# Sparse attention on one core: products with the values issued for two key tiles at a time, with PSUM divided anew

## The chip, the core and the metric

The kernel runs on one of the eight cores of a Trainium2 chip. The metric is the device time of one execution in microseconds. A core has five engines with an instruction queue each: TensorE (PE in the profile; its weight loads are PEld) for matrix products, VectorE (DVE), ScalarE (ACT) and GpSimd (POOL) for work on tiles, and SyncE (SP), which here issues DMAs. Each runs its queue in order and waits at semaphores for the others. TensorE writes its results to PSUM, which here is handed out in eight banks of 128 partitions by 512 float32; the other engines read them from there and free the bank.

## The reference

One inference step of a decoder layer with two head groups: native sparse attention (8 query heads of 64, 2 key/value heads) and a gated DeltaNet, under one norm, one input projection and one output projection. There are 2048 prompt tokens of width 1024 and 8 x 4 sample tokens. For the attention of the prompt, which is where the change is:

```
s  = q_raw . ck / 8 ; p = softmax(s, c_start + 31 <= q_pos) ; o_cmp = p . cv          # compressed blocks
imp = p . overlap ; idx = top_8(imp, first block and the two at the query forced)     # 64-token blocks
o_slc = softmax(q . k over the 8 chosen blocks, causal) . v                           # selected blocks
o_win = softmax(q . k, 0 <= q_pos - k_pos <= 512) . v                                 # sliding window
o = (g0 * o_cmp + g1 * o_slc + g2 * o_win) * silu(z)
```

Every float32 product of the projections and scores is made of split parts; the outputs are float32.

## The kernel before

The program is written with a tile framework: the Python code names tiles and operations, and a scheduler fixes the order of each engine's queue when the kernel is built. It goes by the order in which the code issues the operations, by when operands and buffers are free in its own timing, and it places every semaphore wait. So an order on an engine is the scheduler's, and not always that of the code.

The stages are `project`, `gdn`, `nsa` (the attention) and `outproj`; parts overlap at their edges. `nsa` works through 8 units, `units`: 4 query blocks `qs` of 512 queries times 2 key/value heads `h`. For each unit there are three branches `b` (0 compressed, 1 selected, 2 window) and two pairs `p` of query heads. In branch 1 the selection is not gathered: all keys are scored, and rows of the operand `QHM` carry a large negative number for the blocks that were not chosen and the negative row maximum.

`stream` makes one flat list, `items`, of key tiles `(k, b, p, n, N, x)`: unit, branch, pair, number, count and the key tile of 128 keys with its columns of queries. For an item:

- `score` (lines 1469 to 1497) makes, for each of two heads, a tile pss of PSUM with two matmuls (`scores`, lines 1440 and 1441), and ScalarE takes the exponential into a tile pt of SBUF (line 1482). Where the tile crosses the diagonal or the window's edge, VectorE masks 128 columns (line 1492).
- the product with the values (line 1573) takes pt into the accumulator O, 64 output rows for each head, side by side in the two halves of TensorE's columns. It is a float32 product; the trace shows it in two passes, so a key tile has four rows. The first of the two also waits until both heads' pt are ready.
- pt is added to the pt of the pair's first key tile, on VectorE or GpSimd by the running counts in `busy` (line 1583), for the softmax's sum. After the pair's last key tile ScalarE copies O to oS (line 1587), and `defer` lines up `sums` (tile L) and the `merge` steps, which scale the three branches (tile B, line 1528) and add them on GpSimd (lines 1532 and 1541) some items later.

The scores run `dep` = 1 item ahead of the products. After each item `stream` yields, and the loop at the end of `nsa` issues some steps of `prepare` for the next unit: the compressed branch's maxima and scores (psc, psr), the choice of blocks (psl, psp, psi, tsel), and the maxima that the exponentials need. For these TensorE scores the keys once more, into psm (line 1374, with a mask addition in line 1376), psw (1389 and 1390) and psv (1397 and 1399), and VectorE reduces each to block maxima (lines 1377, 1391 and 1400). At a unit's end `max_end` puts these together (tile wm, lines 1403 to 1406), and `max_rows` transposes wm on TensorE (tile tm, line 1283) and sends it by DMA into rows of `QHM`, before the next unit's scores. Just before the first item of the next unit is scored, `stream` yields "last" and the rest of `prepare` is issued.

PSUM's eight banks are divided by `pb3 = 2, 3, 3`: two for O, three for the scores (pss, psr), three for everything that `X` hands out (psm, psw, psv, psc, psl, psp, psi, tsel, tm, L, B). `npt` = 8 buffers hold pt, `nos` = 9 hold oS.

Of the kernel before, what the change touches and what calls it, by code (L numbers as in the profile page):

```python
# [7 lines left out]
F32 = mybir.dt.float32  # L8
# [3 lines left out]
AF = mybir.ActivationFunctionType  # L12
ALU = mybir.AluOpType
# [91 lines left out]
class K:  # L105
# [1100 lines left out]
    def nsa(self):  # L1206
        nc, tc, i, o = self.nc, self.tc, self.i, self.o
        with ExitStack() as st:
# [262 lines left out]
            def score(u, b, p, item):  # L1471

                kt, c0, c1, mk = item
                if b == 0:
                    return [u["pc"][2 * p], u["pc"][2 * p + 1]]
                out = []
                for g in (2 * p, 2 * p + 1):
                    ps = pS.tile([128, 512], F32, tag="s", name="pss")
                    scores(ps[:, c0:c1], key(KHH, b - 1, u["h"], kt, kt + 1), key(KLM, b - 1, u["h"], kt, kt + 1),
                           u["QHL"][:, g, c0:c1], u["QHM"][:, g, c0:c1])  # L1480
                    pt = wk.tile([128, 512], F32, tag="pt", name="pt", bufs=self.npt)
                    last = nc.scalar.activation(pt[:, c0:c1], ps[:, c0:c1], AF.Exp)  # L1482
# [12 lines left out]

            def sums(u, b, W):

                L = X([128, 512], "L")
                for g in range(4):
                    nc.tensor.matmul(L[32 * g:32 * g + 32, :], self.ones[:, 0:32], W[g], start=True, stop=True, tile_position=(0, 32 * g))  # L1500
                t = wk.tile([128, 512], F32, tag="T", name="T", bufs=1)
                nc.scalar.activation(t, L, AF.Copy)
                nc.sync.dma_start(u["Ld"][b], t[0:128:32, :])
# [41 lines left out]
            def stream():  # L1545

                items = []
                for k, (qs, h) in enumerate(units):
                    for b in range(3):
                        for p in range(2):  # L1550
                            t = tiles_of(qs, b)
                            items += [(k, b, p, n, len(t), x) for n, x in enumerate(t)]
                W = {}

                def ahead(j):
                    if j < len(items):
                        k, b, p, n, N, x = items[j]
                        W[j] = score(U[k], b, p, x)
                for j in range(self.dep):
                    ahead(j)  # L1560
                for j, (k, b, p, n, N, x) in enumerate(items):
                    u = U[k]
                    e = j + self.dep
                    if e < len(items) and items[e][0] != items[e - 1][0]:
                        yield "last", items[e - 1][0]
                    ahead(e)
                    kt, c0, c1, mk = x
                    if n == 0:
                        O = pO.tile([128, 512], F32, tag="O", name="O")
                        acc = W[j]  # L1570
                    val = cvP[:, 64 * u["h"]:64 * u["h"] + 64] if b == 0 else V[b - 1, kt // 4][:, kt % 4, 64 * u["h"]:64 * u["h"] + 64]
                    for gg in range(2):
                        mm = nc.tensor.matmul(O[64 * gg:64 * gg + 64, c0:c1], val, W[j][gg][:, c0:c1], start=(n == 0), stop=(n == N - 1), tile_position=(0, 64 * gg))  # L1573
                        if gg == 0 and len(W[j]) == 3:

                            tc.add_manual_dep(mm.ins, W[j][2].ins.name, mybir.DependencyInfo(mybir.DependencyClass.Sync, mybir.DependencyReason.DATA), reason="both heads at once")
                    if n:
                        for gg in range(2):
                            w = (c1 - c0) / 512
                            tp_, td = 0.1 + self.nb[0] * w, 0.1 + self.nb[1] * w  # L1580
                            e = "p" if busy["p"] + tp_ <= busy["d"] + td else "d"
                            busy[e] += tp_ if e == "p" else td
                            (nc.gpsimd if e == "p" else nc.vector).tensor_tensor(out=acc[gg][:, c0:c1], in0=acc[gg][:, c0:c1], in1=W[j][gg][:, c0:c1], op=ALU.add)  # L1583
                    del W[j]
                    if n == N - 1:
                        S = u["O", b, p] = wk.tile([128, 512], F32, tag="oS", name="oS", bufs=self.nos)
                        nc.scalar.activation(S, O, AF.Copy)
                        u["W", b, p] = acc[:2]
                        if b and p == 1:
                            defer(self.nd[0], lambda u=u, b=b: sums(u, b, u["W", b, 0] + u["W", b, 1]))  # L1590
                        if b == 2 and p == 1:
                            defer(self.nd[1], lambda u=u: merge1(u))
                            defer(self.nd[2], lambda u=u: merge2(u))
                            for pp in range(2):
                                for bb in range(3):
                                    defer(self.nd[3] + 3 * pp + bb, lambda u=u, pp=pp, bb=bb: merge3(u, pp, bb))
                                defer(self.nd[3] + 3 * pp + 3, lambda u=u, pp=pp: merge4(u, pp))
                    tick()
                    yield "step", k
                while later:  # L1600
                    tick()

# [28 lines left out]
                        gen = None  # L1631

    nsa_blocks = range(4)
    pb3 = 2, 3, 3
    dep = 1
    mc = 9.0, 0.0
    npre = 1
    jpre = 0
    nx, ny, npt, nos = 10, 4, 8, 9
    nd = 2, 3, 5, 8  # L1640
    nb = 1.1, 0.5
    whe = 'gpsimd'
# [410 lines left out]
```

## Time and profile before

| | |
|---|---|
| median of 3 runs | 2365.2 us (2360.37 to 2371.74) |
| the profiled execution's own time | 2365.14 us |
| its span, first to last instruction | 2363.4 us |
| mean granted clock of TensorE | 0.958 |
| TensorE busy | 2183.8 us, 92% of the span, 13338 matmuls |
| TensorE's weight loads | 1668.8 us, 71% |
| VectorE busy | 1280.0 us, 54% |
| ScalarE busy | 796.7 us, 34% |
| GpSimd busy | 763.3 us, 32% |

The first product of a pt with values starts at 1249.0 us and the last at 2065.4 us. In the rows below a line begins with its start and duration in us, or with the engine, then the line of the program as L1573, the operation, the tiles as out<-in and the shape. "x4" counts instructions that are put together in a row. Times in brackets are idle time of the engine before the row, and what ended it. Ends of matmuls are modelled, so distances are best read from start to start.

### The profile page before, as it was taken

The page shows a single profiled execution, that of the slowest core. Times are in us where ns is not written, and L with a number is a line of the kernel's source. Part 1 is how long each engine was busy: PE and PEld are TensorE (multiplying, and loading weights), DVE is VectorE, ACT ScalarE, POOL GpSimd, SP SyncE. Part 2 cuts the span into 40 slices and gives each one's busy share as a digit, 9 for nine tenths or more (in the row PEclk, how much of TensorE's full clock was granted, in tenths as well). Part 3 has the DMA queues.
Part 4 walks back from the last instruction along what each step waited for, and adds up shares of the span by engine and source line. Part 5 has one row for each costly group of instructions (what it writes and reads, how often), then busy time and mean ns, then how long its engine had stood idle before and what let it go on. Part 6 is the DMA issues. An engine that isn't in the chain of part 4 may idle for free. (4 is left out here: it accounts for less than half of the span.)

```text
span 2363.4 us, 36125 instructions
## 1 busy us (share of the span) xinstructions
PE 2183.8 (92%) x13338; PEld 1668.8 (71%) x13340; DVE 1280.0 (54%) x2660; ACT 796.7 (34%) x1688; POOL 763.3 (32%) x957
## 2 busy tenths in 40 slices
PE   4999989999999899996793899999999999999998
PEld 4999888999999888996682455455455453477765
DVE  4300135566521266566551578687768787844542
ACT  4411224332214133453351324334343444522221
POOL 2104211111100004512141246455464655422742
PEclk9999999999999899998796989998999999999999
DMA  8432331124442464546638342232122102384652
GB/s 244 130 83 93 100 106 63 59 69 81 119 145 87 141 179 128 157 128 150 138 104 169 62 83 52 35 67 53 39 47 39 28 6 60 93 241 145 197 189 94
DMA packets 304467, 248.12 MB, mean 105 GB/s; under 512 B 106039, under 2 KB 260835, under 8 KB 301987
## 3 DMA queue, kind: packets, MB, share of 16 engines
q1 hardware_dynamic: 282923, 194.53, 32.2%
q0 software_dynamic: 7424, 33.56, 4.2%
q10 hardware_dynamic: 13944, 17.72, 2.6%
q8 instruction: 105, 1.72, 0.3%
q14 instruction: 71, 0.58, 0.1%
HBM read 173.60 MB, written 74.42 MB: 105 GB/s over the span
## 5 line engine op out<-in xcount | busy, mean ns | idle before, releaser
L1583 POOL TENSOR_TENSOR pt<-pt 128x512 f32<-128x512 f32 (+3 forms) x332 | 320.6, 977 | 371.4 <-DVE pt L1492 178.9
L1482 ACT ACTIVATE pt<-pss 128x512 f32<-128x512 f32 (+3 forms) x544 | 254.8, 494 | 383.9 <-PE pss L1441 204.4
L1573 PE MATMUL O<-pt,V 128*64 128x512 f32 (+3 forms) x1088 | 243.1, 527 | 10.9 <-DVE pt L1492 10.9
L1377 DVE TENSOR_REDUCE bm<-psm 128x8 f32<-128x512 f32 (+3 forms) x320 | 189.6, 603 | 66.3 <-PE psm L1374 49.5
L1440 PE MATMUL pss<-qhl,khh 128*128 128x512 f32 (+3 forms) x544 | 218.6, 407 | 1.2 <-ACT pt L1482 0.6
L1440 PEld LDWEIGHTS pss<-qhl,khh 128*128 128x128 f32 x544 | 105.4, 194 | 135.9 <-issue 97.2
L1441 PE MATMUL pss<-qhm,klm 98*128 98x512 f32 (+3 forms) x544 | 191.8, 361 | 5.4 <-DMA qhl<-rl 4.0
L261 PE MATMUL ps<-xhi,whi 128*128 128x416 f32 x880 | 191.0, 359 | 2.5 <-ACT sb L514 2.5
L261 PE MATMUL ps<-xhi,wlo 128*128 128x416 f32 x880 | 189.7, 355 | 0.0
L261 PE MATMUL ps<-xlo,whi 128*128 128x416 f32 x880 | 187.6, 354 | 0.0
L261 PEld LDWEIGHTS ps<-xhi,whi 128*128 128x128 f32 x880 | 166.7, 191 | 15.9 <-issue 4.7
L261 PEld LDWEIGHTS ps<-xlo,whi 128*128 128x128 f32 x880 | 166.1, 189 | 2.1
L261 PEld LDWEIGHTS ps<-xhi,wlo 128*128 128x128 f32 x880 | 165.7, 189 | 1.9
L1492 DVE TENSOR_TENSOR pt<-pt,caps 128x128 f32<-128x128 f32 x349 | 138.1, 415 | 21.1 <-ACT pt L1482 19.9
L1374 PE MATMUL psm<-khh,qhl 128*128 128x512 f32 (+3 forms) x320 | 129.0, 416 | 18.0 <-DMA qhl<-ql 11.5
L1583 DVE TENSOR_TENSOR pt<-pt 128x512 f32<-128x512 f32 (+3 forms) x148 | 122.8, 839 | 32.7 <-PE O L1573 17.4
L466 DVE SCALAR_TENSOR_TENSOR acc<-cx,wc,acc 128x416 f32<-128x416 f32 (+1 forms) x180 | 124.1, 690 | 4.6
L1441 PEld LDWEIGHTS pss<-qhm,klm 98*128 98x128 f32 x544 | 106.4, 197 | 17.0 <-DMA qhl<-rl 4.9
L1573 PEld LDWEIGHTS O<-pt,V 128*64 128x64 f32 x1088 | 55.9, 137 | 85.6 <-issue 33.3
L239 DVE TENSOR_TENSOR wlo<-wraw,whi 128x1024 fp32r<-128x1024 f32 x30 | 35.7, 1223 | 146.1 <-ACT whi L238 133.9
L1391 DVE TENSOR_REDUCE ww<-psw 128x1 f32<-128x512 f32 (+3 forms) x128 | 80.9, 632 | 51.7 <-PE psw L1390 50.9
L1374 PEld LDWEIGHTS psm<-khh,qhl 128*128 128x128 f32 x320 | 62.0, 198 | 57.2 <-issue 16.6
(506 smaller groups left out, 4150.3 us busy)
## 6 DMA issues: line engine op xcount, KB each, us to landing
kq<-qkvt SPq DMA_DIRECT2D x64, 256.0 KB
qkvt<-acc SPq DMA_DIRECT2D x60, 208.0 KB
wraw<-w_in SPq DMA_DIRECT2D x24, 512.0 KB
xt<-x_prompt SPq DMA_DIRECT2D x16, 512.0 KB
m<-mx SPq DMA_DIRECT2D x16, 512.0 KB
x<-x_prompt ACTq DMA_DIRECT2D x16, 512.0 KB
out<-y SPq DMA_DIRECT2D x16, 512.0 KB
qh<-hi SPq DMA_DIRECT2D x20, 208.0 KB
```

The source lines that it names most:

```text
L239: nc.vector.tensor_tensor(out=wlo[:, :, c:c + m], in0=raw, in1=whi[:, :, c:c + m].bitcast(F32), op=ALU.subtract)
L261: nc.tensor.matmul(ps, x, y, start=(k == 0), stop=(k == 23))
L466: nc.vector.scalar_tensor_tensor(acc[:, :n], cx[:, j:j + n], wc[:, j, c:c + 1], acc[:, :n], op0=ALU.mult, op1=ALU.add)
L1374: nc.tensor.matmul(ps[:, 0:128 * (b - a)], QHL[:, g, 128 * s:128 * s + 128], key(KHH, 0, h, a, b), start=True, stop=not diag)
L1377: nc.vector.tensor_reduce(out=bm[:, s, g, 2 * a:2 * b], in_=ps[:, 0:128 * (b - a)].rearrange("p (n k) -> p n k", k=64), axis=AX.X, op=ALU.max)
L1391: nc.vector.tensor_reduce(out=ww[:, g, s, 0:1], in_=ps[:, 0:128 * (e - a)], axis=AX.X, op=ALU.max)
L1440: nc.tensor.matmul(ps, lhs1, r1, start=True, stop=False)
L1441: nc.tensor.matmul(ps, lhs2, r2, start=False, stop=True)
L1482: last = nc.scalar.activation(pt[:, c0:c1], ps[:, c0:c1], AF.Exp)
L1492: last = nc.vector.tensor_tensor(out=x, in0=x, in1=caps[:, int(nm == "neglow")], op=ALU.min)
L1573: mm = nc.tensor.matmul(O[64 * gg:64 * gg + 64, c0:c1], val, W[j][gg][:, c0:c1], start=(n == 0), stop=(n == N - 1), tile_position=(0, 64 * ...
L1583: (nc.gpsimd if e == "p" else nc.vector).tensor_tensor(out=acc[gg][:, c0:c1], in0=acc[gg][:, c0:c1], in1=W[j][gg][:, c0:c1], op=ALU.add)
```

## The change

`items` is cut into `groups` of up to `grp` = 2 key tiles of the same unit, branch and pair. The scores of group m + 1 are issued, then the products of group m: all of its products follow each other, and the first one waits until every pt of the group is ready. Then the adds, the copies of O, the deferred steps and the steps of `prepare` follow, item by item as before. The division of PSUM goes from 2, 3, 3 to 2, 4, 2: a fourth bank for scores, and two instead of three for what `X` hands out. There are 10 buffers for pt instead of 8, and 7 for oS instead of 9.

```diff
-                for j in range(self.dep):
-                    ahead(j)
-                for j, (k, b, p, n, N, x) in enumerate(items):
...
-                    ahead(e)
...
-                    for gg in range(2):
-                        mm = nc.tensor.matmul(O[64 * gg:64 * gg + 64, c0:c1], val, W[j][gg][:, c0:c1], start=(n == 0), stop=(n == N - 1), tile_position=(0, 64 * gg))
-                        if gg == 0 and len(W[j]) == 3:
...
+                groups = []
+                for j, x in enumerate(items):
+                    if groups and x[:3] == items[groups[-1][0]][:3] and len(groups[-1]) < self.grp:
+                        groups[-1].append(j)
+                    else:
+                        groups.append([j])
+
+                def ahead(n):
+                    if n < len(groups):
+                        for j in groups[n]:
+                            k, b, p, _, N, x = items[j]
+                            W[j] = score(U[k], b, p, x)
+
+                def values(js):
+                    nonlocal O, acc
+                    first, waits = None, [W[j][2] for j in js if len(W[j]) == 3]
+                    for j in js:
...
                         for gg in range(2):
+                            mm = nc.tensor.matmul(O[64 * gg:64 * gg + 64, c0:c1], val, W[j][gg][:, c0:c1], start=(n == 0), stop=(n == N - 1), tile_position=(0, 64 * gg))
+                            if first is None:
+                                first = mm
+
+                                for w in waits:
+                                    tc.add_manual_dep(mm.ins, w.ins.name, mybir.DependencyInfo(mybir.DependencyClass.Sync, mybir.DependencyReason.DATA), reason="both heads at once")
+
+                O = acc = None
+                ahead(0)
+                for m, js in enumerate(groups):
+                    if m + 1 < len(groups) and items[groups[m + 1][0]][0] != items[js[-1]][0]:
+                        yield "last", items[js[-1]][0]
+                    ahead(m + 1)
+                    values(js)
+                    for j in js:
...
-    pb3 = 2, 3, 3
-    dep = 1
+    pb3 = 2, 4, 2
+    grp = 2
...
-    nx, ny, npt, nos = 10, 4, 8, 9
+    nx, ny, npt, nos = 10, 4, 10, 7
```

The adds, the copy of O and the deferred steps are the same lines as before, moved behind `values(js)`. What the scheduler made of it on TensorE stands in four pieces. The first is the kernel before, in the window branch of the last query block, where the key tiles cross the diagonal (a number behind a tile's name only tells tiles of one name apart; in brackets are the engines whose semaphores a matmul waits for):

```order
L1573 MATMUL O<-pt,V_11718 64x512 [waits DVE_49]
L1573 MATMUL O<-pt,V_11718 64x512
L1440 MATMUL pss<-qhl_11700,khh_11715 128x256 [waits Activation_49]
L1441 MATMUL pss<-qhm_11701,klm_11716 128x256
L1397 LDWEIGHTS identb
L1397 MATMUL psv<-tri_11745,identb 128x512 [waits DVE_49]
L1399 MATMUL psv<-khh_11711,qhl_11706 128x128 x4
L1440 MATMUL pss<-qhl_11700,khh_11715 128x128 [waits Activation_49]
L1441 MATMUL pss<-qhm_11701,klm_11716 128x128
L1374 MATMUL psm<-khh_11699,qhl_11706 128x512 [waits DVE_49]
L1374 MATMUL psm<-khh_11705,qhl_11706 128x512 [waits DVE_49]
L1573 MATMUL O<-pt,V_11718 64x384 [waits DVE_49]
```

In it one key tile's products stand between the scores of others. The same place in the kernel after:

```order
L1581 MATMUL O<-pt,V_11718 64x512 [waits DVE_49]
L1581 MATMUL O<-pt,V_11718 64x512
L1581 MATMUL O<-pt,V_11718 64x384 x2
L1440 MATMUL pss<-qhl_11700,khh_11711 128x128 [waits Activation_49]
L1441 MATMUL pss<-qhm_11701,klm_11712 128x128
L1374 MATMUL psm<-khh_11711,qhl_11706 128x512 [waits DVE_49]
L1332 MATMUL psl<-pc,ones 32x512 [waits DVE_49]
L1332 MATMUL psl<-pc,ones 32x512 x3
L1440 MATMUL pss<-qhl_11700,khh_11711 128x256 [waits Activation_49]
L1441 MATMUL pss<-qhm_11701,klm_11712 128x256
```

Here the products of two key tiles, 512 and 384 columns wide, stand in a row, and the preparation's psm and psl between the scores. The third piece is the end of the fifth of the eight units, where the last steps of `prepare` for the sixth stand (tm from wm is the very last), in the kernel before:

```order
L1441 MATMUL pss<-qhm_11701,klm_11708 128x384
L1440 MATMUL pss<-qhl_11700,khh_11705 128x384 [waits Activation_49]
L1441 MATMUL pss<-qhm_11701,klm_11708 128x384
L1440 MATMUL pss<-qhl_11700,khh_11705 128x512 [waits Activation_49]
L1441 MATMUL pss<-qhm_11701,klm_11708 128x512
L1573 MATMUL O<-pt,V_11710 64x128 [waits DVE_49]
L1573 MATMUL O<-pt,V_11710 64x128
L1573 MATMUL O<-pt,V_11710 64x256 [waits DVE_49]
L1573 MATMUL O<-pt,V_11710 64x256
L1440 MATMUL pss<-qhl_11700,khh_11705 128x512 [waits Activation_49]
L1441 MATMUL pss<-qhm_11701,klm_11708 128x512
L1283 MATMUL tm<-ident,wm 32x128 [waits DVE_49,PE_49]
```

Scores and three key tiles' products of the unit stand right ahead of tm. The fourth is the same end in the kernel after:

```order
L1374 MATMUL psm<-khh_11711,qhl_11706 128x512 [waits DVE_49]
L1376 LDWEIGHTS identb
L1376 MATMUL psm<-neglow,identb 128x128
L1365 MATMUL tsel<-ident,imp 32x128 [waits DVE_49]
L1365 MATMUL tsel<-ident,imp 32x128 x3
L1389 MATMUL psw<-khh_11711,qhl_11706 128x512 [waits DVE_49]
L1390 LDWEIGHTS identb
L1390 MATMUL psw<-neglow,identb 128x128
L1397 LDWEIGHTS identb
L1397 MATMUL psv<-tri_11745,identb 128x512 [waits Activation_49]
L1399 MATMUL psv<-khh_11705,qhl_11706 128x128 x4
L1283 MATMUL tm<-ident,wm 32x128 [waits DVE_49,PE_49]
```

There the last preparation tiles, psm, tsel, psw, psv, stand in a row with tm and with no scores or products between them.

## Rows read from the trace of the kernel before

**Rows 1.** Table by stages: the attention, and ten of its microseconds.

```profile
core 0: us, PE busy (x) PEld busy (x) DVE busy (x) ACT busy (x) POOL busy (x), PEclk, DMA share, GB/s
1300.00:2066.00 766.00, 729.87 (x3507) 378.43 (x3506) 590.10 (x1170) 303.09 (x639) 387.29 (x390) 0.96 0.24 51
1498.00:1508.00 10.00, 9.55 (x30) 4.93 (x31) 3.42 (x6) 2.77 (x5) 0.04 (x1) 0.51 0.26 39
```

**Rows 2.** TensorE's timeline, one key tile's products alone (start us, duration us).

```profile
1652.48 0.40 PE L1441 MATMUL pss<-qhm,klm 98*128 98x512 f32 x1
1652.72 0.39 PE L1374 MATMUL psm<-khh,qhl 128*128 128x512 f32 x1
1653.04 1.08 PE L1573 MATMUL O<-pt,V 128*64 128x512 f32 x4
1654.05 0.50 PE L1440 MATMUL pss<-qhl,khh 128*128 128x512 f32 x1
1654.39 0.40 PE L1441 MATMUL pss<-qhm,klm 98*128 98x512 f32 x1
```

**Rows 3.** Waits of TensorE in the attention (us in total, times, longest).

```profile
PE psm L1374 <- DMA qhl<-ql: 11.2, 5, 4.1
PE O L1573 <- DVE pt L1492: 6.6, 10, 3.2
...
PE psm L1374 <- DVE ww L1391: 3.7, 1, 3.7
...
PE tm L1283 <- DVE wm L1406: 2.0, 3, 0.9
PE psm L1374 <- DVE bm L1377: 1.6, 4, 0.7
```

**Rows 4.** Waits of its weight loads in the attention.

```profile
PEld pss L1440 <- ACT pt L1482: 30.8, 55, 0.8
...
PEld psm L1374 <- DVE bm L1377: 15.0, 25, 1.7
...
PEld psm L1374 <- DVE ww L1391: 8.3, 9, 4.0
...
PEld tm L1283 <- DVE wm L1406: 4.6, 3, 1.8
```

**Rows 5.** TensorE's timeline, two key tiles' products in a row.

```profile
1694.72 1.08 PE L1573 MATMUL O<-pt,V 128*64 128x512 f32 x4
1695.63 1.03 PE L1573 MATMUL O<-pc,cvP 128*64 128x512 f32 x4
1696.59 0.33 PE L1440 MATMUL pss<-qhl,khh 128*128 128x128 f32 x1
```

**Rows 6.** Timeline of all engines, two preparation tiles and their reductions.

```profile
1693.43 0.23 PE L1376 MATMUL psm<-neglow,identb 128*128 128x128 bf16 x1
...
1693.70 0.69 DVE L1377 TENSOR_REDUCE bm<-psm 128x8 f32<-128x512 f32 x1 [0.42 <-PE psm L1376]
...
1694.31 0.68 DVE L1391 TENSOR_REDUCE ww<-psw 128x1 f32<-128x512 f32 x1
1694.39 0.40 PE L1374 MATMUL psm<-khh,qhl 128*128 128x512 f32 x1
...
1695.10 0.69 DVE L1377 TENSOR_REDUCE bm<-psm 128x8 f32<-128x512 f32 x1
```

**Rows 7.** Timeline of all engines at the end of a unit.

```profile
1827.07 0.68 DVE L1400 TENSOR_REDUCE ww<-psv 128x4 f32<-128x512 f32 x1
...
1828.47 0.49 DVE L1406 TENSOR_SCALAR wm<-wm 128x32 f32<-128x32 f32 x1
...
1829.02 0.28 PE L1283 MATMUL tm<-ident,wm 128*32 128x128 f32 x1 [0.49 <-DVE wm L1406]
```

**Rows 8.** TensorE's timeline, its wait for the next queries.

```profile
1498.45 0.79 PE L1374 MATMUL psm<-khh,qhl 128*128 128x512 f32 x1 [4.09 <-DMA qhl<-ql]
```

**Rows 9.** The merges' adds on GpSimd (ns min/median/max).

```profile
L1532 POOL TENSOR_TENSOR oS<-oS x32: 1265/1282/2252, 1378.3 to 2098.2; 128x512 f32<-128x512 f32 x32
```

More of the change, by code (lines that the diff above doesn't have):

```diff
@@ L1553, in stream @@
                 W = {}
-                def ahead(j):
-                    if j < len(items):
-                        k, b, p, n, N, x = items[j]
-                        W[j] = score(U[k], b, p, x)
-                for j in range(self.dep):
-                    ahead(j)
-                for j, (k, b, p, n, N, x) in enumerate(items):
[L1562 to L1565, printed above, removed]
-                    ahead(e)
[L1567 to L1571, printed above, removed]
-                    for gg in range(2):
-                        mm = nc.tensor.matmul(O[64 * gg:64 * gg + 64, c0:c1], val, W[j][gg][:, c0:c1], start=(n == 0), stop=(n == N - 1), tile_position=(0, 64 * gg))
-                        if gg == 0 and len(W[j]) == 3:
-                            tc.add_manual_dep(mm.ins, W[j][2].ins.name, mybir.DependencyInfo(mybir.DependencyClass.Sync, mybir.DependencyReason.DATA), reason="both heads at once")
-                    if n:
-                        for gg in range(2):
[L1579 to L1599, printed above, removed]
@@ new lines, in values @@
+                def values(js):
+                    nonlocal O, acc
+                    first, waits = None, [W[j][2] for j in js if len(W[j]) == 3]
+                    for j in js:
+                        k, b, p, n, N, x = items[j]
+                        u = U[k]
+                        kt, c0, c1, mk = x
+                        if n == 0:
+                            O = pO.tile([128, 512], F32, tag="O", name="O")
+                            acc = W[j]
+                        val = cvP[:, 64 * u["h"]:64 * u["h"] + 64] if b == 0 else V[b - 1, kt // 4][:, kt % 4, 64 * u["h"]:64 * u["h"] + 64]
+                        for gg in range(2):
+                            mm = nc.tensor.matmul(O[64 * gg:64 * gg + 64, c0:c1], val, W[j][gg][:, c0:c1], start=(n == 0), stop=(n == N - 1), tile_position=(0, 64 * gg))
[3 more added lines that the diff above has]
+                                    tc.add_manual_dep(mm.ins, w.ins.name, mybir.DependencyInfo(mybir.DependencyClass.Sync, mybir.DependencyReason.DATA), reason="both heads at once")
@@ new lines, in stream @@
+                O = acc = None
[6 more added lines that the diff above has]
+                    for j in js:
+                        k, b, p, n, N, x = items[j]
+                        u = U[k]
+                        kt, c0, c1, mk = x
+                        if n:
+                            for gg in range(2):
+                                w = (c1 - c0) / 512
+                                tp_, td = 0.1 + self.nb[0] * w, 0.1 + self.nb[1] * w
+                                e = "p" if busy["p"] + tp_ <= busy["d"] + td else "d"
+                                busy[e] += tp_ if e == "p" else td
+                                (nc.gpsimd if e == "p" else nc.vector).tensor_tensor(out=acc[gg][:, c0:c1], in0=acc[gg][:, c0:c1], in1=W[j][gg][:, c0:c1], op=ALU.add)
+                        del W[j]
+                        if n == N - 1:
+                            S = u["O", b, p] = wk.tile([128, 512], F32, tag="oS", name="oS", bufs=self.nos)
+                            nc.scalar.activation(S, O, AF.Copy)
+                            u["W", b, p] = acc[:2]
+                            if b and p == 1:
+                                defer(self.nd[0], lambda u=u, b=b: sums(u, b, u["W", b, 0] + u["W", b, 1]))
+                            if b == 2 and p == 1:
+                                defer(self.nd[1], lambda u=u: merge1(u))
+                                defer(self.nd[2], lambda u=u: merge2(u))
+                                for pp in range(2):
+                                    for bb in range(3):
+                                        defer(self.nd[3] + 3 * pp + bb, lambda u=u, pp=pp, bb=bb: merge3(u, pp, bb))
+                                    defer(self.nd[3] + 3 * pp + 3, lambda u=u, pp=pp: merge4(u, pp))
+                        tick()
+                        yield "step", k
```

## The prediction

> **What bounds the kernel now.** I read three views. First the table by stages [rows 1]: the attention, from 1300 to 2066 us, shows TensorE busy for 730 of 766 us, VectorE for 590, GpSimd for 387, ScalarE for 303. So TensorE sets this stage, and VectorE, at 77%, is the engine with the least room behind it. Second the timeline of TensorE in a quiet stretch [rows 2]: a busy share near 1 is not a full engine there. Two score matmuls of 512 columns start 0.23 to 0.24 us apart. Around the products with the values the steps are longer: the last 128-column matmul starts at 1652.72 and the products at 1653.04 (0.32 us, where 0.235 would do), the four rows of the products last until 1654.05 (1.01 us), and the next score takes 0.34 us until its successor starts. (The two products of a key tile lie side by side in the two column halves; each runs in two passes, hence four rows.) Third the waits of TensorE and of its weight loads [rows 3, 4]. A weight load that stands idle beside a streaming matmul costs nothing, so these are upper ends: the loads waited 30.8 us for score banks, 23.3 us for banks of the preparation's tiles (15.0 + 8.3), 4.6 us for wm. TensorE itself waited only 5.3 us for those preparation banks (3.7 + 1.6), 11.2 us for the next queries' DMA and 6.6 us for masked tiles.
>
> **The change, part by part.** All sums stand against the profiled execution, 2365.1 us (span 2363.4 and 1.7 us around it), practically the median of the runs, 2365.2.
>
> *Fewer changes between scores and values.* The order of TensorE has 576 products with the values, before and after. Before they stand in 269 uninterrupted groups, 248 of them of one key tile; after in 138, 115 of them of two (the first two pieces of the order show one place). The price of a group is what lies around its streaming. In [rows 5] two key tiles follow each other by chance: from 1694.72 to 1696.59, 1.87 us, against 2 x 1.01 = 2.02 alone [rows 2], so 0.15 us goes inside. Entry 0.32 - 0.235 = 0.085 and exit 0.34 - 0.235 = 0.105 go with it: 0.34 us a group. It is a fixed time and not one per column, so narrow diagonal tiles save it too. 131 groups x 0.34 = **-45 us**. This is the surest term.
>
> *Four score banks for three, products a pair behind.* A score's bank is free when its exponential is done, and with the products of the pair before in between, that wait should go. It is worth between 0 (TensorE's own wait for it is not among the rows that matter) and -31 (the loads' whole 30.8 us). The wait for masks, 6.6 us, may shrink or, since the first product of a pair now waits for four tiles, grow. Together I take **-8**, nearer to zero because most of a load's idle time is beside a matmul.
>
> *Two banks for three in the preparation of the next unit.* This is what pays for the fourth score bank. psm, psw and psv are score tiles whose block maxima VectorE reduces; a new one needs the bank of the tile two (before: three) places back. The price from the rows [rows 6]: a tile whose mask addition starts on TensorE at 1693.43 is reduced from 1693.70 to 1694.39. With nothing ahead on VectorE, a full-width tile so costs 0.40 (matmul) + 0.04 + 0.69 = 1.13 us from its start, 0.9 us beyond its own slot of 0.235, and about 0.95 until TensorE reacts (the last 0.05 is my estimate from the 0.04 us hop). With work ahead it takes longer: the tile started at 1694.39 is reduced from 1695.10 to 1695.79, behind the reduction of 0.68 us and a mask: 1.40 us from its start, 1.2 beyond its slot. I then walked TensorE's order in the attention and added up, between each preparation matmul that waits for VectorE and the matmul whose reduction it waits for, the TensorE work at these row durations (a wait already taken counted as cover for the next). Before, 3 of 510 such waits have under 0.45 us of cover and 18 have 0.45 to 0.95. After, 65 of 523 have under 0.45 (mean 0.26) and 82 have 0.45 to 0.95 (mean 0.73). At 0.95 us: 65 x 0.69 + 82 x 0.22 = 63, less 6 before: +57. At 1.2 us: 65 x 0.94 + 82 x 0.47 = 100, less 11: +89. If VectorE is always as quick as its shortest row allows and the hop is free, 0.8: +40. I take 1.0: 65 x 0.74 + 82 x 0.27 = 70, less 7: **+63**. The before side checks the size: its 6 to 11 us agree with TensorE's own 5.3 us in [rows 3], and are under the loads' 23.3.
>
> The Trainium skill, Perfetto Trace Analysis, section Matmuls, asks that independent matmul groups rotate through different PSUM banks so that the evacuation of one overlaps the next. It speaks for the score side and against the preparation side, and gives no price; by it alone, with no term for the groups, the sum would be -8 + 63 = +55, 2420 us. Both kernels use eight banks, so the rule does not say which side wins; the rows above do.
>
> *End of a unit.* The last two pieces of the order show the largest knot: before, 14 score matmuls and three key tiles' products stand between the last preparation tile and tm, the transpose that needs wm; after, the preparation's last tiles and tm stand in one row with nothing between. Before, such work covered most of the chain, here at another unit's end [rows 7]: psv is reduced at 1827.07, wm is ready at 1828.96, tm starts at 1829.02 after 0.49 us of waiting. After, nothing covers these 2 us at 7 units: 14 us, of which the count of banks above already holds 6, and 6.6 (2.0 + 4.6) were waited before in part. I take **+7**, between 0 and +14. The next wait, for the queries' DMA [rows 3], has its transfer issued as before; where TensorE idled 4.09 us for it, its granted clock was 0.51 in the 10 us after, so nearly all of them at the lower level of 1.2 GHz [rows 1, 8], and that is in both kernels. I leave it at 0, +5 at most.
>
> *pt 8 to 10, oS 9 to 7, adds.* The adds are the same 480, split 332 to 148 as before, and GpSimd has half its time free. The order now lets the copy of a unit's second O wait for the previous unit's merge; ScalarE, at 40%, and the second O bank cover it. 0, and +30 at the bad end (third rival).
>
> Sum: -45 - 8 + 63 + 7 = +17: **2382 us**. With the bounds of the terms alone: -45 - 31 + 40 + 0 = -36 (2329) up to -45 + 0 + 89 + 14 + 5 = +63 (2428).
>
> **Rivals.**
> *The drain wins (2336).* The short covers may stand where TensorE would wait anyway: at the unit's end behind the DMA wait of 11.2 us, or where scores wait for pt. Then the bank term is some +25 in place of 63: -45 - 8 + 25 = -28, 2337. For it: the surest term is the gain, and with fewer tiles ahead VectorE's queue is shorter. Against: the 65 shortest covers are spread through the order, several to a unit, and VectorE is already 77% busy.
> *The two cancel (2365).* Banks at 0.8 us (+40), nothing at the unit's end, scores -8, drain -45: -13 to 0.
> *GpSimd's merges hold the exponentials (2412).* Two pairs of two heads need 8 pt, and sums of one or both halves 2 to 4 more; there are 10. In the second half the third and fourth exponential of a pair so wait for adds of the pair before, and these stand on GpSimd behind a unit's merges, four of 1.28 us [rows 9] and two products of the same size, some 7.7 us. If half of that reaches TensorE at 8 units, +30 comes on top: 2412. It decides once GpSimd runs more than six tiles behind; against it, two pts more are there, and GpSimd is busy for only 387 of the 766 us.
>
> **How the numbers follow.** About 12 us, 0.5%, is what a measurement tells from no change. The forecast (2370 to 2400) gets 0.45, of which 0.10 lies under 2377. The drain's victory gets 0.27, the tie 0.12, the merges 0.16. So faster 0.27, same 0.10 + 0.12 = 0.22, slower 0.35 + 0.16 = 0.51. The range 2333 to 2420 takes in most of both outer cases and is near the bounds of the terms; the forecast's own range is 2370 to 2400.
>
> **What would show it.** Right: rows of products x8 in TensorE's timeline, some 130 exits of 0.34 us fewer, so about 45 us less of matmul steps without a wait; waits of psm, psw and psv for bm and ww up from 5 to some 50 us or more on TensorE and its loads together; idle time at tm near 2 us a unit; VectorE idle more often behind PE psm. Wrong: if those bank waits stay under 30 us, the kernel is faster; if they are there but the pairs save less than 0.2 us each, it is worse than said; if ScalarE waits tens of us for GpSimd's pt, the third rival holds. Outside 1100 to 2066 us nothing should move by more than a few us.

## The result and the profile after

The changed kernel takes 2431.6 us (median of four runs, 2423.9 to 2442.6), the kernel before 2365.9 (2360.4 to 2371.7): ratio 1.0291, 95% interval 1.0258 to 1.0324. That is 66 us slower. 2382 was forecast, and the range ended at 2420: the direction was right, the size was not. In the profiled executions it is 2432.1 against 2365.1. Of these 67 us, 62 lie between the start of the second unit and the last product with the values; before and behind it the two traces differ by 1 to 3 us each, as forecast.

The table by stages [rows 1] now reads as follows; the second row is a short piece of it.

```profile
core 0: us, PE busy (x) PEld busy (x) DVE busy (x) ACT busy (x) POOL busy (x), PEclk, DMA share, GB/s
1300.00:2131.00 831.00, 754.13 (x3505) 416.92 (x3504) 616.38 (x1170) 288.80 (x639) 390.88 (x388) 0.90 0.21 46
1614.50:1631.50 17.00, 15.08 (x46) 9.13 (x45) 9.21 (x19) 5.30 (x10) 0.65 (x2) 0.51 0.10 17
```

The stage is longer, TensorE is idle for 77 us of it against 36, and its granted clock is 0.90 on average where it was 0.96. The busy columns hide the gain, since a matmul at the lower level is busy for longer (0.79 us in [rows 8], 0.39 for the same form in [rows 2]). So I took TensorE's matmul starts from the traces and compared each distance from one start to the next with the 10th percentile of the same kind of step (same shapes in front and behind) at the full clock, over all kernels of this study. The sum of these percentiles is the column "steps"; what a step took beyond that in a stretch of granted clock 0.5, up to twice its length, is "low clock"; all else is "waits". All numbers are us, from the start of the second unit to the last product. Some matmul records are missing from each trace, so a few us either way mean nothing. The line between steps and waits also depends on what counts as the same kind: with the shape of one more matmul in front as a part of it (the longer kind in what follows), the difference below is -37, +36 and +62.

| kernel | stage | steps | low clock | waits |
|---|---|---|---|---|
| before | 745 | 612 | 25 | 108 |
| changed | 807 | 559 | 56 | 192 |
| difference | +62 | -53 | +31 | +84 |
| forecast | +17 | -45 | 0 | +62 |

The steps came near the forecast by either count (-53 or -37 for -45), and here is a pair of key tiles in TensorE's timeline [rows 2, 5]:

```profile
1760.43 0.39 PE L1441 MATMUL pss<-qhm,klm 98*128 98x512 f32 x1
1760.75 1.94 PE L1581 MATMUL O<-pt,V 128*64 128x512 f32 x8
1762.62 0.74 PE L1374 MATMUL psm<-khh,qhl 128*128 128x512 f32 x2
```

Entry 0.32, eight rows in 1.87 us, as in the one case by chance from which the price was taken; 36 full pairs of the changed kernel have a median of 1.868. (x8 counts four rows for each of the two key tiles.)

The waits of TensorE [rows 3] and of its weight loads [rows 4], from 1300 to 2130 us (us in total, times, longest):

```profile
PE O L1581 <- DVE pt L1492: 19.3, 17, 5.4
PE psm L1374 <- DVE bm L1377: 11.5, 24, 1.3
PE tm L1283 <- DVE wm L1406: 11.5, 6, 2.3
PE psm L1374 <- DVE ww L1391: 4.9, 13, 0.5
...
PE psw L1389 <- DVE bm L1377: 3.3, 8, 1.0
```

```profile
PEld O L1581 <- DVE pt L1492: 30.2, 33, 5.5
PEld psm L1374 <- DVE bm L1377: 29.9, 53, 1.5
PEld pss L1440 <- ACT pt L1482: 24.5, 40, 1.7
...
PEld psm L1374 <- DVE ww L1391: 16.2, 26, 0.9
```

TensorE's own waits for preparation banks went from 5.3 us to 20 (the rows of psm and psw above; more small groups lie under them), tm's from 2.0 to 11.5, both the way that was forecast. Of the 5.3 us, 3.7 were a single stop, and its length came from a DMA. The reduction that frees the bank stood on VectorE behind a step that waited for one (kernel before, all engines):

```profile
1312.47 0.25 DVE L1339 RECIPROCAL r<-r 128x16 f32<-128x16 f32 x1 [5.01 <-DMA r<-Ld]
1312.64 0.49 DVE L1391 TENSOR_REDUCE ww<-psw 128x1 f32<-128x384 f32 x1
...
1313.19 0.80 PE L1374 MATMUL psm<-khh,qhl 128*128 128x512 f32 x1 [3.74 <-DVE ww L1391]
```

The products' wait for masked tiles, which was to shrink, went from 6.6 to 19.3.

What the lost bank does is best seen where TensorE works through preparation tiles with little between (all engines; a number in brackets is idle time and its releaser):

```profile
1612.37 0.23 PE L1376 MATMUL psm<-neglow,identb 128*128 128x128 bf16 x1
...
1612.55 0.68 DVE L1377 TENSOR_REDUCE bm<-psm 128x8 f32<-128x512 f32 x1
...
1613.28 0.49 PE L1389 MATMUL psw<-khh,qhl 128*128 128x512 f32 x1 [0.69 <-DVE bm L1377]
...
1613.46 0.68 DVE L1377 TENSOR_REDUCE bm<-psm 128x8 f32<-128x512 f32 x1
...
1614.20 0.49 PE L1374 MATMUL psm<-khh,qhl 128*128 128x512 f32 x1 [0.35 <-DVE bm L1377]
1614.22 0.68 DVE L1391 TENSOR_REDUCE ww<-psw 128x1 f32<-128x512 f32 x1
```

Each tile starts when VectorE has reduced the tile two places back, so TensorE goes at VectorE's pace, a tile every 0.76 to 0.92 us, and idles 0.3 to 0.7 us in each. Just behind these rows, at 1614.8, the granted clock falls, for 17.1 us (the second row of the table by stages: 0.51, the level of 1.2 GHz). In the stage there are 21 such stretches with 167 us in sum; before there were 7 with 65 us. Just ahead of ten of the 21 stand two or more steps of 0.58 to 1.07 us into preparation tiles, as here; three more begin during a wait for wm, and three during waits of products in the last unit.

And the end of a unit [rows 7]:

```profile
1871.82 0.74 PE L1399 MATMUL psv<-khh,qhl 128*128 128x128 f32 x4
1874.84 0.37 PE L1283 MATMUL tm<-ident,wm 128*32 128x128 f32 x1 [2.28 <-DVE wm L1406]
```

Nothing is in front of tm now, and TensorE waits out VectorE's reduction of psv and the two steps behind it, 2.3 us.

### The profile page after: what moved, and what is told of

Read it like the earlier page. It is cut to its first block, busy times and chain, and to the rows that moved or that the text cites. A ratio compares the mean times of both kernels' runs of the same rounds, so it can differ in the third digit from the quotient of the medians.

```text
span 2430.1 us, 36067 instructions
## 1 busy us (share of the span) xinstructions
PE 2208.8 (91%) x13338; PEld 1710.7 (70%) x13340; DVE 1307.3 (54%) x2660; ACT 781.8 (32%) x1688; POOL 766.2 (32%) x957
## 4 chain that ended last, share of the span: by engine, by line
PE 59%; DVE 13%; DMA 7%; issue 3%; SPq 2%; ACT 2%; POOL 2%; ACTq 0%; POOLq 0%; DVEq 0%
PE ps L261 17%; PE ps L1983 6%; PE O L1581 5%; PE u L1176 4%; PE pss L1440 3%; PE pss L1441 3%; DVE pt L1492 3%; DVE bm L1377 3%; PE psm L1374 2%; DVE pt L1605 2%; POOL pt L1605 1%; PE psw L1389 1%; PE tp L1161 1%; DMA out<-er 1%; DVE ww L1391 1%
## 5 line engine op out<-in xcount | busy, mean ns | idle before, releaser
L1605 POOL TENSOR_TENSOR pt<-pt 128x512 f32<-128x512 f32 (+3 forms) x332 | 326.4, 1002 | 321.4 <-DVE pt L1492 158.7
L1482 ACT ACTIVATE pt<-pss 128x512 f32<-128x512 f32 (+3 forms) x544 | 243.1, 496 | 362.9 <-PE pss L1441 119.3
L1581 PE MATMUL O<-pt,V 128*64 128x512 f32 (+3 forms) x1088 | 222.2, 534 | 23.8 <-DVE pt L1492 23.7
L1440 PE MATMUL pss<-qhl,khh 128*128 128x512 f32 (+3 forms) x544 | 206.8, 388 | 4.2 <-ACT pt L1482 4.2
L1492 DVE TENSOR_TENSOR pt<-pt,caps 128x128 f32<-128x128 f32 x349 | 154.2, 469 | 86.5 <-ACT pt L1482 85.9
L1374 PE MATMUL psm<-khh,qhl 128*128 128x512 f32 (+3 forms) x320 | 145.2, 472 | 31.3 <-DVE bm L1377 21.8
L1581 PEld LDWEIGHTS O<-pt,V 128*64 128x64 f32 x1088 | 69.3, 143 | 126.8 <-issue 83.7
L1605 DVE TENSOR_TENSOR pt<-pt 128x512 f32<-128x512 f32 (+3 forms) x148 | 132.5, 907 | 36.0 <-POOL pt L1605 18.9
L249 PE MATMUL ps<-whi,xhi 128*128 128x256 f32 (+3 forms) x544 | 81.5, 293 | 19.5 <-ACT whi L238 14.9
```

Source lines behind the costliest of these rows:

```text
L1374: nc.tensor.matmul(ps[:, 0:128 * (b - a)], QHL[:, g, 128 * s:128 * s + 128], key(KHH, 0, h, a, b), start=True, stop=not diag)
L1440: nc.tensor.matmul(ps, lhs1, r1, start=True, stop=False)
```

## The experiments

Ratios are to the kernel before in runs on the same chip, with the 95% interval; times are medians. The columns steps, low clock and waits of each profiled run are in a table at the end of the section. "Before" and "changed" name the kernel that was edited.

### Which half of the change costs: e1 to e4

e1 is before with the banks of the changed kernel alone (first edit); e2 is changed with the banks of before (second):

```diff
-    pb3 = 2, 3, 3
+    pb3 = 2, 4, 2
```

```diff
-    pb3 = 2, 4, 2
+    pb3 = 2, 3, 3
```

> The kernel before with PSUM divided 2, 4, 2 and nothing else: the products stay in groups of one key tile. Theory A (the preparation's two banks cost the time, partly as waits for VectorE and partly as stretches at the lower granted clock that these bring): slower than before by some 50 us of waits and 20 to 30 us of clock, 2430 to 2455 us, and low-clock time in the attention well over the 68 us of before. Theory B (the pairing costs it: a pair's products wait for four exponentials, and pts are held too long): within 10 us of before, 2356 to 2376.

Measured: 2429.4 us, ratio 1.0261 (1.0234 to 1.0288), that is +62 us. Theory A holds, and the forecast's +63 for the banks looks exact. It is so by two errors that cancel: waits grew by 38 us, not by the 70 that banks and tm together were given, and low clock by 25, not by 0.

> The changed kernel with PSUM divided 2, 3, 3 as before; pairs, 10 pt and 7 oS as changed. Theory A: the saving on groups without its price, 45 us off before: 2315 to 2335 us, waits of psm and psw for VectorE as before, low-clock time under 90 us. Theory B: slower than before, 2390 or more, with TensorE waiting at O for masked pt and ScalarE for GpSimd's pt as in the changed kernel.

Measured: 2360.4 us, ratio 0.9985 (0.9972 to 0.9998). The bank cost is gone, and theory B with it. But theory A's size failed too: the steps are 44 us shorter (41 with the longer kind), as forecast, and only 5 us of them reach the end. This is the finding that the rest of the study follows.

e3 takes the fourth score bank from O (changed, `pb3 = 1, 4, 3`); e4 is the changed kernel with `grp = 1`, so key tile by key tile with its banks and pt:

> The changed kernel with PSUM divided 1, 4, 3: the fourth score bank is taken from O instead of the preparation. Theory A: the saving on groups less 48 waits for the copy of O (0.6 us each, some covered): 2325 to 2350 us. Theory B: 2390 or more. Against e2 it tells what the fourth score bank is worth.

Measured: 2398.7 us, ratio 1.0150 (1.0127 to 1.0172). It is under the changed kernel, so a third preparation bank is worth more than the second O. It is over theory A's 2350 and inside theory B's "2390 or more"; since e2 has ruled out B, the likely reason is the single O, whose next products wait for its copy, with exponentials held up as well (ScalarE waits 85.1 us for GpSimd's pt). No run tells these two apart.

> The changed kernel with groups of one key tile (grp = 1), PSUM 2, 4, 2, 10 pt and 7 oS: everything of the change but the pairs. Theory A: the price without the saving, 2430 to 2460 us, above the changed kernel's 2432 by up to 30. Theory B: 2356 to 2385.

Measured: 2422.3 us, ratio 1.0254 (1.0214 to 1.0294): the banks alone, again, and somewhat under theory A's 2430 to 2460. From here to the changed kernel the pairs take 40 us of steps away and add 9 us of low clock and 34 of waits.

### VectorE's reductions: e5 to e8

```diff
-  in_=ps[:, 0:128 * (b - a)].rearrange("p (n k) -> p n k", k=64)
+  in_=ps[:, 0:16 * (b - a)].rearrange("p (n k) -> p n k", k=8)
```

The edit is that of psm; psw's is like it, over an eighth of its columns. e5 is before with it, e6 the changed kernel with it, e7 the changed kernel with it and `pb3 = 2, 3, 3`.

> The kernel before, with VectorE's reductions of psm and psw over an eighth of their columns (the block maxima and row maxima are taken from those few columns only; all else is as before). It takes some 200 us of VectorE's 590 us in the attention away (296 reductions of 0.62 us and 105 of 0.68 us become short ones). Theory A (the changed kernel pays at banks that VectorE has yet to reduce): before waits there for only some 6 us, so the kernel gains little from it by itself, 2320 to 2360 us, and serves as the base for the next two. Theory B (the banks are not what pays) expects the same here.

> The changed kernel with the same short reductions as e5. Theory A (the price of two preparation banks is VectorE's reduction before a bank is free, and the lower clock that follows the waits): with a reduction of some 0.15 us in place of 0.62 to 0.69 a bank is free before TensorE has gone through the 0.24 us of the next tile and its own, the waits shrink from 49 + 22 us (psm, psw) to under 20, and the distance to e5 falls from +66 us to between -30 and +15 us. Theory B (what costs is the pairing itself, the pt tiles held for it, or the issue order at a unit's end): the distance to e5 stays over +40 us.

> Pairs with the banks of before (2, 3, 3), with the same short reductions as e5. It asks why pairs with three preparation banks gained only 4 us (2360.4 against 2365.6) where their matmul steps are 41 us shorter. Theory C (VectorE is next in line: with TensorE quicker, its masks, adds and reductions, 600 of 740 us, end last and the saving turns into waits): with 200 us of VectorE's work gone the saving shows, and this kernel is 30 to 45 us under e5. Theory D (the saving is lost in what pairs themselves add, the wait of a pair's first product for the exponentials and masks of two key tiles and for pt, whatever VectorE's load): within 15 us of e5.

Measured: e5 2362.2 us, ratio 0.9998 (0.9973 to 1.0024); e6 2365.6, ratio 1.0020 (1.0005 to 1.0034); e7 2347.8, ratio 0.9927 (0.9898 to 0.9956). e6 is 3.5 us over e5 where the changed kernel is 66 over before, as theory A expected. The banks by themselves are seen where both kernels have pairs and only the banks differ: the changed kernel is 71 us over e2, e6 is 18 over e7. So most of the price of two banks, some 50 of 71 us, is the time that VectorE takes to empty them; 18 us stay, and no run shows why. The waits behind the banks are cut as well (e6, 1300 to 2060 us):

```profile
PE psm L1374 <- DVE bm L1377: 5.7, 6, 2.2
...
PE psw L1389 <- DVE bm L1377: 0.9, 3, 0.5
```

and the low clock with them, from 56 us to 35. e7 gains 14 us on e5 (17 by the ratios): far from theory C's 30 to 45 and at the edge of theory D's "within 15", so VectorE's load is a part of the answer to e2 and no more.

e8 is e2 with the pt and oS of before (`npt, nos = 8, 9`):

> Pairs with banks 2, 3, 3 as in e2, but with the 8 pt and 9 oS tiles of before in place of 10 and 7. A pair of key tiles takes four pt, the pair ahead four more, and an accumulator keeps its own two: 8 should be tight. Theory D (pt tiles are what holds pairs up): 20 us or more over e2, 2380 us and up, with ScalarE's wait for pt from GpSimd well over e2's. Theory C (VectorE): within 12 us of e2's 2360.

Measured: 2379.6 us, ratio 1.0078 (1.0055 to 1.0102), some 22 us over e2 by the two ratios, as theory D expected. Pairs need the ten pt: the loads' wait for score banks is 50.2 us in place of 25.6, since exponentials find no pt.

### The masks: e9 to e12

e9 (before) and e10 (changed, `pb3 = 2, 3, 3`) leave the masks of pt out (349 on VectorE and 3 on GpSimd in the trace of before). With the masks gone, the running counts also give 21 more of the 480 adds to GpSimd, in both kernels alike:

```diff
-                    for c, nm in mk:
+                    for c, nm in ():
```

> The kernel before, without VectorE's masks of the exponentials on the diagonal and at the window's lower edge (340 operations of 0.42 us are left out, so those tiles attend to keys that the reference masks). Base for e10. Theory E (in pairs, the first product waits for the masks of two key tiles, which stand on VectorE behind adds and reductions; one by one the masks are mostly covered): little change here, 2335 to 2362 us. Theory D (the pairs' loss lies with pt tiles and bursts of scores, whatever the masks): the same here.

> Pairs with banks 2, 3, 3 (as e2), without VectorE's masks, as in e9. Theory E: the waits of products for masked tiles (17 us on TensorE in e2, 6 before) are gone, and the pairs gain 25 to 45 us against e9. Theory D: no more than 10 us against e9.

Measured: e9 2358.1 us, ratio 0.9986 (0.9970 to 1.0002); e10 2335.2, ratio 0.9899 (0.9865 to 0.9933). 23 us of the pairs' 50 us of steps come through, against 5 with the masks: theory E in kind, a little short of its 25 at least. In e2 one wait for masks looks like this (all engines, its last unit):

```profile
1976.49 0.28 PE L1441 MATMUL pss<-qhm,klm 98*128 98x256 f32 x1
...
1978.46 1.35 DVE L1492 TENSOR_TENSOR pt<-pt,caps 128x128 f32<-128x128 f32 x1
...
1979.84 0.69 DVE L1605 TENSOR_TENSOR pt<-pt 128x512 f32<-128x512 f32 x1
1980.45 0.48 DVE L1492 TENSOR_TENSOR pt<-pt,caps 128x128 f32<-128x128 f32 x2
1980.86 1.22 DVE L1969 TENSOR_TENSOR wol<-wor,woh 128x1024 fp32r<-128x1024 f32 x1
1981.99 0.55 DVE L1605 TENSOR_TENSOR pt<-pt 128x384 f32<-128x384 f32 x1
...
1982.46 0.89 DVE L1492 TENSOR_TENSOR pt<-pt,caps 128x128 f32<-128x128 f32 x4
...
1982.80 3.25 PE L1581 MATMUL O<-pt,V 128*64 128x512 f32 x8 [4.50 <-DVE pt L1492]
```

The first product of a pair needs the masks of four tiles; on VectorE they stand between adds (L1605) and even a step that prepares the output projection's weights (L1969), and in the last unit no preparation fills the 4.5 us.

e11 and e12 are e2 with the rule for a pair edited; e11 first, e12 second:

```diff
-if groups and x[:3] == items[groups[-1][0]][:3] and len(groups[-1]) < self.grp:
+if groups and x[0] < len(units) - 1 and x[:3] == items[groups[-1][0]][:3] and len(groups[-1]) < self.grp:
```

```diff
-if groups and x[:3] == items[groups[-1][0]][:3] and len(groups[-1]) < self.grp:
+if groups and not x[5][3] and not items[groups[-1][0]][5][3] and x[:3] == items[groups[-1][0]][:3] and len(groups[-1]) < self.grp:
```

> Pairs with banks 2, 3, 3 (as e2), but key tile by key tile in the last unit, where no preparation is left to lie between: there e2 stood idle 4.6, 3.2, 2.5 and 1.9 us for masked tiles (before: 3.3 and 1.0), and its last unit took 112.0 us against 107.8. 20 of the pairs go, worth 7 us of steps; the waits should fall by some 8 us. Theory E: 2350 to 2360 us, level with e2 or a few us under it. Theory D: over e2 by the lost pairs, 2363 to 2370 us.

Measured: 2344.7 us, ratio 0.9931 (0.9908 to 0.9955), some 13 us under e2 by the two ratios and faster than either kernel of the case. The last unit takes 100.4 us in place of 112.0, and low clock falls from 31 to 22 us. That is more than theory E expected.

> Pairs with banks 2, 3, 3 (as e2), but a key tile with a mask stands alone; only pairs of tiles without masks are left (60 of 123). Each keeps its saving of 0.34 us, 20 us in all against the kernel before, and no product waits for the masks of two tiles. Theory E: 2335 to 2352 us, faster than before and than e2. Theory D: 2358 to 2368 us, since half of the saving is gone and the rest is lost as in e2.

Measured: 2360.7 us, ratio 1.0004 (0.9986 to 1.0022). Theory E fails here and theory D's number holds (2358 to 2368): pairs without any masked tile keep 18 us of shorter steps and gain nothing (low clock +11, waits +10).

### How much would come through at all, and the small terms: e13 to e18

e13 and e14 join the edits of e5 and e9 (and of e7 and e10); e15 is e11 with `ny` 6 for 4; e16 and e17 are before with `npt, nos = 10, 7` and `8, 7`; e18 is e11 with `9, 8`.

> The kernel before without VectorE's masks and with the short reductions, both (as e5 and e9 together: block and row maxima from an eighth of the columns, masks left out). VectorE's work in the attention falls by 300 us. Base for e14. Neither alone moved the time by over 3 us, so 2350 to 2362 us; theory C and theory F expect the same here.

> Pairs with banks 2, 3, 3 (as e2) with both reliefs of e13. Theory C+E (the saving of 41 us in matmul steps is real, and what eats it are waits for VectorE, masks and reductions together): 30 to 42 us under e13. Theory F (a part is lost in the pairs' own bursts, score banks waiting for exponentials, and in a lower granted clock that has nothing to do with VectorE): 10 to 25 us under e13.

Measured: e13 2351.5 us, ratio 0.9948 (0.9929 to 0.9968); e14 2339.6, ratio 0.9901 (0.9868 to 0.9935). The gap is 12 us (the two intervals just touch): theory F. The profiled executions lie further apart, 16 us, with 20 in the stage. In them the pairs have 56 us less of steps and 31 us more of waits; of these 18 are score tiles (pss, 16 to 34 us), which a pair asks for in a row of four. With the longer kind it is 41 less and 14 more, 11 of them at pss.

> e11 with the preparation planned to end six steps ahead of a unit's end in place of four (ny 6 for 4). In TensorE's order tm then has scores or products before it at all but one unit's end, where in e11 nothing stands between psv and tm at three. Theory G (each uncovered wm costs its 2.6 us, and the lower clock behind it as much again): 6 to 12 us under e11. Rival (the wait only moves, to the next queries' DMA behind tm): within 4 us of e11.

Measured: 2352.9 us, ratio 0.9951 (0.9931 to 0.9971), some 5 us over e11 by the ratios. tm's waits fell only from 8.8 to 6.1 us, and single stops at other places grew. Theory G missed; the rival's 4 us lie within the noise of the two ratios. The price of tm alone isn't settled by it.

> The kernel before with 10 pt and 7 oS tiles for 8 and 9, all else as before, key tile by key tile. e11's last unit, key tile by key tile too, took 100.4 us against 107.8 before. If ten pt are what helped there, this kernel's last unit is near 100 too and it gains 5 to 9 us on before; if not, it is within 4 us of before and e11's gain belongs to the pairs in the units ahead.

> The kernel before with 7 oS tiles for 9, pt left at 8. TensorE's order before tm is as before (scores and products cover wm). If the oS tiles cost the 10 us of e16 (copies of O held up by merges): 2370 to 2376 us, and ScalarE's wait for GpSimd's oS is near 20 us. If the pt tiles do, by the uncovered wm: within 4 us of before.

Measured: e16 2374.9 us, ratio 1.0043 (1.0025 to 1.0062); e17 2366.0, ratio 1.0014 (0.9995 to 1.0034). Both expectations of e16 missed: it is slower than before by 10 us, and its last unit takes 106.6 us, not 100. e17 meets the second of its own: the missing oS cost nothing that can be measured, so the two more pt cost the time, some 7 us between the two runs (whose intervals overlap a little). In e16 the scheduler leaves tm bare at places, as here (TensorE's timeline):

```profile
1831.87 0.74 PE L1399 MATMUL psv<-khh,qhl 128*128 128x128 f32 x4
1835.29 0.37 PE L1283 MATMUL tm<-ident,wm 128*32 128x128 f32 x1 [2.68 <-DVE wm L1406]
```

TensorE's waits for wm are 5.4 us in e16 and 1.9 in e17 (from 1320 us on), so this is about half of the 7 us; where the rest goes is open.

> e11 (pairs with banks 2, 3, 3 in all units but the last) with 9 pt and 8 oS for 10 and 7. Eight pt cost pairs 19 us (e8 against e2). If pairs need the tenth: 2350 to 2360 us. If the second pair of oS is worth more: under e11's 2345.

Measured: 2363.8 us, ratio 0.9997 (0.9978 to 1.0017), some 16 us over e11 by the ratios, more than the 2350 to 2360 expected of a missing tenth pt. Pairs need it; single key tiles do better without (e16, e17).

The split of each profiled run, in us:

| kernel | stage | steps | low clock | waits |
|---|---|---|---|---|
| e1 banks alone | 811 | 615 | 50 | 146 |
| e2 pairs, old banks | 741 | 568 | 31 | 142 |
| e3 pairs, 1, 4, 3 | 775 | 565 | 38 | 171 |
| e4 items, new banks and pt | 805 | 599 | 47 | 158 |
| e5 / e7 short reductions, items / pairs | 746 / 730 | 619 / 570 | 21 / 31 | 105 / 129 |
| e6 changed, short reductions | 749 | 564 | 35 | 150 |
| e8 pairs, 8 pt | 763 | 571 | 37 | 156 |
| e9 / e10 no masks, items / pairs | 741 / 722 | 619 / 569 | 21 / 35 | 101 / 117 |
| e11 pairs, not the last unit | 728 | 575 | 22 | 131 |
| e12 pairs, masked alone | 748 | 594 | 36 | 118 |
| e13 / e14 light VectorE, items / pairs | 732 / 712 | 627 / 571 | 16 / 22 | 89 / 120 |

## Why the prediction was wrong

- **The pairs' saving, -45: this step failed.** "This is the surest term" was said of the steps, and they are near enough: -53 in the changed kernel, -44 in e2 (-37 and -41 with the longer kind). But the sum took a step saved for time saved. With the banks of before they give 5 us (e2), with the new ones none (the changed kernel is 9 us over e4). In place of the gain stand more waits and some low clock. Where they come from is shown in parts, which overlap: 18 us come back with VectorE's masks gone (23 us of gain in e10 over e9, 5 in e2), 13 with the last unit alone (e11 against e2), 9 with its reductions shortened (14 in e7 over e5, 5 in e2). With masks gone and reductions short, both, 12 us come through (e14 against e13), so VectorE isn't all of it. e12 shows the same without masked pairs. The reading that fits these runs is that TensorE sets the stage on average, but another engine is just behind at many of its stops, and what it saves it waits for there; which engine at which stop is shown for the masks only.
- **Score banks and masks, -8: wrong in sign.** The waits at pss fell by 2 us (30 to 28 in the split), those at O rose by 16 (22 to 38); in TensorE's own rows, masked tiles alone went from 6.6 to 19.3. The text had the reason, a first product that waits for four tiles, and gave it no price; [rows 3] showed a longest wait of 3.2 us for masked tiles in before, and the order of VectorE's queue in the last unit could have been priced.
- **Two preparation banks, +63: right in sum, wrong inside.** e1 has +62 for the banks alone, and e6 against e7 shows that VectorE's emptying is most of the cause. The waits are smaller than the 1.0 us of the forecast made them: with psm, psw, psv and B +51 in the changed kernel. The rest is the clock. That the working's 6 to 11 us for before agreed with the 5.3 in [rows 3] was luck: 3.7 of these were the stop behind a DMA at 1313 us.
- **The clock, "I leave it at 0, +5 at most": failed.** +31 in the changed kernel, +25 with the banks alone. [Rows 8] had it, a wait and 0.51 behind it; I asked only whether that one wait would grow, and not what trains of half-idle tiles do. Without it the range ended at 2420.
- **End of a unit, +7: right**, +10 in the split (13 against 3), 9.5 in the waits' rows. That the ten pt may do a part of it (5.4 us at wm in e16) was put at 0.
- **The rivals.** The drain's victory and the tie are out. The third has its sign: ScalarE waits for GpSimd's pt and oS as it said (changed kernel):

```profile
ACT pt L1482 <- POOL pt L1605: 63.3, 55, 3.8
ACT oS L1609 <- POOL oS L1532: 63.3, 12, 21.6
```

  But e6 has nearly as much,

```profile
ACT pt L1482 <- POOL pt L1605: 59.0, 50, 4.0
ACT oS L1609 <- POOL oS L1532: 40.2, 10, 14.8
```

  and is within 4 us of e5, so these waits are mostly off the path and don't carry the 66 us. e7, 18 us under e6, has only 21.9 and 23.7 of them, so a part of these 18 us may be theirs.

Put together: -53 for -45 is 8 us to the good; +31 of clock and 22 us of waits more than forecast, 16 of them at O, are the miss, with 5 us outside the stage. By the experiments it is simpler: the new banks cost the 62 us that they were forecast to cost, and of the pairs' 45 us nothing came.

The Trainium skill, Perfetto Trace Analysis, section Matmuls, wants independent matmul groups to rotate through PSUM banks so that emptying one overlaps the next. It gives no price, and the runs agree with it. In e1 it is 62 us for the third bank of a rotation whose emptying takes up to 0.69 us a tile on a busy VectorE, less what the fourth score bank gives. With pairs it is 71 us, and 18 once the emptying is short (e6 against e7).

What stays open: what stands behind the waits of e14 beyond the score tiles, the 18 us between e6 and e7, the price of an uncovered wm by itself, and what the fourth score bank is worth alone. Where the clock falls was read from traces; no run changed the clock alone, so that the paced tiles make it fall is a reading, not shown.

## What to carry to other kernels

Price a saving on the engine that sets the stage twice: by its steps, and by what stands just behind them; here 44 us of shorter steps were worth 5, and 37 were worth 16 once the pairs were left out of the one unit in which no other work fills the waits (e11, the fastest that still computes what the reference asks for). Count the banks of a rotation by the reader's time for a tile, queue included, not by the writer's. And where a change makes TensorE go at another engine's pace for some us, look in the trace of before for the granted clock behind its waits, and carry that into the sum and the range.

## What was not expected of the hardware

- The granted clock fell to 0.51 in stretches in which TensorE shows as busy for 15.08 of 17 us (the second row of the table by stages): tiles paced by VectorE at 0.76 to 0.92 us stood ahead of it, and no stop of over 0.7 us.
- The clock's price and the waits' price come together: e2 has four waits of 1.8 to 4.5 us for masked tiles and four stretches of granted clock 0.5 in its last unit. e11 has no such wait over 1.6 us and no such stretch there, and its low clock cost 9 us less.
- More buffers made a kernel slower: ten pt for eight cost some 7 us key tile by key tile (e16 against e17; 10 against before), while pairs lose 16 to 22 us without them (e18, e8).
